# Five sums made ahead for the first feed-forward in place of eight, two of them for its first pieces, and three more for the second

## The chip, the cores and the metric

The kernel runs on one core of one Trainium2 chip. The metric is the device time of one execution in microseconds (us); lower is better. The profile's engines are TensorE (PE, its weight loads PEld), VectorE (DVE), ScalarE (ACT), GpSimd (POOL) and SyncE (SP). In this kernel SP starts the loads of weights, and POOL starts the transfers that store or fetch intermediate tensors and those that add into their target.

## The reference

One layer of a streaming encoder on 256 tokens of width 2048, all in float32. D_FF is 5632.

```python
x = x + 0.5 * swiglu(rms_norm(x), w_up1, w_down1)      # first feed-forward: FFN1
h = rms_norm(x); proj = h @ w_in                       # the middle
...                                                    # HGRN2 and RG-LRU branches, gates, out projection
x = x + cross_attention(rms_norm(x), rms_norm(mem), wq, wkv, wo)
x = x + 0.5 * swiglu(rms_norm(x), w_up2, w_down2)      # second feed-forward: FFN2
return rms_norm(x)

def swiglu(h, w_up, w_down):
    gate, up = split(h @ w_up, 2)
    return (silu(gate) * up) @ w_down
```

The keys and values of the cross attention depend on `mem` alone (256 tokens) and are computed first of all.

## The kernel before

**Split numbers.** Each float32 operand is split into a high part `h` (a copy rounded to the fast matmul type, by ScalarE, line 147) and a low part `l` (the operand minus `h`, by VectorE, line 148). A product takes three matmuls: high x high, low x high, high x low.

**Pieces.** Weights come in tiles of 128 x 2048 (1 MB), called pieces here, in one planned order: 16 pieces for the memory's values, 16 for its keys (the stage K, lines 367 and 370), FFN1, the middle, FFN2. `weights()` prepares pieces two ahead of the one in use: SP loads `raw` (three buffers, a fourth, `raw1`, in FFN1), ScalarE makes `h`, VectorE makes `l`.

**A feed-forward** has 11 groups. A group has 8 pieces of the up projection; between groups stand pieces of the down projection (two after groups 1 and 2, four after each later one). When a group ends, its sums are evicted, and its results are transposed (line 643) a few pieces later.

**Fast pieces.** Over the blocks of an up piece a Strassen-like scheme with 7 products (21 matmuls) is used in place of 8. It needs four sums of the piece's blocks, each 128 x 512: `td`, made by VectorE in lines 334, 336 and 338, then split to `th` and `tl`. A letter in the table PIECES says how a piece is prepared:

- `f`: raw is loaded, VectorE makes the sums and both low parts.
- `a`: as `f`, but the low part `l` of raw is made by ScalarE (minus raw, line 343) and by a transfer of POOL that adds the piece to it (line 344, `l<-wu`).
- `r`: the sums have been made ahead and lie in device memory. SP loads three quarters of raw (line 317) and the stored sums (line 322, `td<-t`), and VectorE makes only low parts.

The digit is the piece's number in the group. A fifth kind, "fast early", is an `f` whose sums are put into other buffers (`slot`, and raw itself), since the pool `wide` (four buffers, for `td` and `tl`) lies over the tiles of the stages before it.

**Sums made ahead.** `make_ahead` has two steps: POOL loads a piece into a buffer `prep` (line 208); some pieces later VectorE makes the sums in place (line 213, four instructions of 128 x 512) and POOL stores them (line 214). `beside(i)` runs at each prepared piece i and says when each step comes: a new load every third piece, the sums two pieces behind it. There is one `prep` buffer in the stages before FFN1, two or three in the middle, where FFN2's sums are made.

The engines' queues are in order. A scheduler fixes the order of instructions on each engine when the kernel is built, so a wait at the head of a queue holds all that stands behind it.

Of the kernel before, what the change touches and what calls it, by code (L numbers as in the profile page):

```python
# [19 lines left out]
NG = DFF // 512  # L20
# [22 lines left out]


PIECES = "f1 a3 f0 a4 f2 a5 a6 f7"
FIRST = [PIECES.replace("f2", "r2") if g in (1, 2, 4, 5, 6, 7, 8, 9) else PIECES for g in range(NG)]


def first(g):
    return [("fast", g, int(e[1])) for e in FIRST[g].split()]  # L50


def ffn_order(every=False):

    out = [("mixed" if p > 5 else "fast", 0, p) for p in range(8)] if every else first(0)  # L60
    down = [("down", 0, 1, c, 0) for c in range(4)]
    for g in range(1, NG):
        if every:
            out += [("fast", g, p) for p in (1, 3, 4, 0, 2, 5, 6, 7)]
        else:
            out += first(g)
        if g > 2 and g % 2:
            down = [("down", g - 2, 2, c, b) for c in range(4) for b in (g - 2, g - 1)]
        n = 2 if g < 3 else 4
        out, down = out + down[:n], down[n:]  # L70
    return out + [("down", NG - 2, 2, c, b) for c in range(4) for b in (NG - 2, NG - 1)]


def adds(name, e):

    return name == "ffn1" and e[0] == "fast" and f"a{e[2]}" in FIRST[e[1]]


def sums_ready(name, e):

    if name == "ffn1":
        return e[0] == "fast" and f"r{e[2]}" in FIRST[e[1]]
    made = {0: (), 1: (5, 7), 2: (3, 5, 7), 3: (3, 5, 7)}.get(e[1], (0, 3, 5, 7))
    return name == "ffn2" and e[0] == "fast" and e[2] not in made


# [1 line left out]
def block_kernel(ctx: ExitStack, tc: tile.TileContext, xT, xin, memT, vec, gfin, bgate, lruw, wu1, wd1, win, wv,  # L88
# [54 lines left out]
    done = {}  # L143
# [10 lines left out]
    plan, ahead, made_ahead, made_first = [], [], [], []  # L154
    orders = {"ffn1": ffn_order(), "ffn2": ffn_order(every=True)}

    def plan_ffn(name, wu, wd):
        for e in orders[name]:
            src = wd[e[4], e[3]] if e[0] == "down" else wu[e[1], e[2]]
            kind = "fast" if e[0] == "fast" else "plain"  # L160
            if e[0] == "down" and 0 < e[4] < NG - 1 and e[4] % 2 == 0 and e[3] % 2:
                kind = "added"
            if adds(name, e) and e not in orders[name][:2]:
                kind = "fast added"
            if kind == "fast" and (e[1] < 4 if name == "ffn2" else e in orders[name][:2]):
                kind = "fast early"
            if sums_ready(name, e):
                kind = "ready"
                t = kept.tile([P, 2048], F32, name=f"t{e[1]}_{e[2]}")
                (made_first if name == "ffn1" else made_ahead).append((src, t))  # L170
                src = src, t
            plan.append(((name,) + e, src, kind))
# [9 lines left out]
    plan_columns("k", wk, range(KT))  # L182
    first_ffn = len(plan)
    plan_ffn("ffn1", wu1, wd1)
    first_middle = len(plan)
    for hf in range(2):
# [11 lines left out]
    for g, kq in OUT_ORDER:  # L198
        plan.append((("o", g, kq), wo[g, kq], "plain"))
    first_second = len(plan)  # L200
    plan_ffn("ffn2", wu2, wd2)

    head, rest = [], {}

    def make_ahead(src, to):

        t = scoped["prep"].tile([P, 2048], F32, name="prep", tag="prep")
        nc.gpsimd.dma_start(t, src)
        yield
        b = [t[:, i * 512:(i + 1) * 512] for i in range(4)]  # L210
        with tc.issue_after(done["low"]):
            for o, x, y in ((1, 0, 1), (0, 0, 2), (2, 2, 1), (3, 3, 2)):
                dve.tensor_tensor(out=b[o], in0=b[x], in1=b[y], op=ALU.subtract)  # L213
        nc.gpsimd.dma_start(to, t)
        yield

    under_way = []

    def beside(i):

        if under_way and (i >= under_way[0][0] or "prep" not in scoped):
            next(under_way.pop(0)[1])
        if "prep" not in scoped or i < turn[0]:
            return
        if i < first_ffn:
            if made_first:
                turn[0] = i + 3 if len(made_first) > 1 else first_middle + 2
                steps = make_ahead(*made_first.pop(0))
                next(steps)
                under_way.append((i + 2, steps))  # L230
        elif made_ahead and i < first_second - 4:
            early = "scores" in scoped
            turn[0] = i + (3 if early or len(made_ahead) % 3 else 2)
            steps = make_ahead(*made_ahead.pop(0))
            next(steps)
            under_way.append((i + (2 if early or "kt" in scoped else 3), steps))

    turn = [8]
# [3 lines left out]
    def weights(*key):  # L242
        while plan and len(ahead) < 2:
            i = next(planned)
            k, src, kind = plan.pop(0)
            if i == 0:
                in_turn.enter_context(tc.manual_schedule(engines={sp.engine, act.engine, dve.engine}))
            if i == 0:
                begun.append(raw_tile())
                act.dma_start(begun[0][:, :512], in_blocks(src, 512)[:P])  # L250
            if i < len(head):
                head[i]()
            if plan and plan[0][2] == "added":
                begun.append(begin_added(plan[0][1]))
            ahead.append((k, prepare(src, kind, i if i < 4 else None)))
            if i in rest:
                rest[i]()
            beside(i)
            if i == 7:
                in_turn.close()  # L260
        k, w = ahead.pop(0)
        assert k == key, (k, key)
        return w
# [356 lines left out]
    def ffn(name, pairs, sq, then, begin=(), sums=()):  # L620
# [38 lines left out]
        for at, e in enumerate(order):  # L659
# [3 lines left out]
            if kind != "down":  # L663
# [3 lines left out]
                for i, (a, b, n) in enumerate(PRODUCTS["ready" if sums_ready(name, e) else kind]):  # L667
                    u = uses[g, n]
                    if u[0] == (p, i):
                        accs[n] = bank()  # L670
                    own, less = pairs[p]
                    products.append((accs[n], part(own, a, P) if a >= 0 else part(less, -1 - a, P), part(w[b // 4] if fast else w, b % 4, 512),
                                     u[0] == (p, i), u[-1] == (p, i)))
# [798 lines left out]
```

## Time and profile before

| | us |
|---|---|
| median of 3 runs (2517.64 to 2519.73) | 2519.39 |
| the profiled execution | 2521.97 |
| its span, from the first to the last instruction | 2520.2 |
| TensorE busy in the span | 2423.2 |
| VectorE busy in the span | 2100.6 |
| K, from its first product to FFN1's first | 99.8 to 213.1 |
| FFN1, to the last group's transposes | 213.1 to 910.7 |
| middle and FFN2 | 910.7 to 2520.2 |

A row of the profile's instructions gives the start, the duration, the engine, the line, the operation, what it writes and reads, a count, and in brackets how long the engine was idle before it and what ended that idle time. Buffer numbers are left out of names there: `td<-t` is any load of stored sums. A row of a table by stage gives for each engine its busy time and its instructions, then the clock granted to TensorE (1.00 is full), the share of time that the 16 DMA engines were busy, and their rate.

### The profile page before, as it was taken

To read this page: it belongs to the slowest core of one execution; us is meant where nothing else is said; L and a number is where in the kernel's file an instruction comes from. 1 tells how busy PE (TensorE), PEld (TensorE's weight loads), DVE (VectorE), ACT (ScalarE), POOL (GpSimd) and SP (SyncE) were. 2 spreads that over 40 slices of the span, in tenths; PEclk is the share of its full clock that TensorE was granted. 3 is DMA by queue.
4 is the path that set the end of the run, shared out by engine and by line. 5 is a ranking of instruction groups with operands and counts; after the bars stand their busy time and mean duration, and the time that the engine had idled before them with its cause. 6 is when DMAs were issued, how large, how long until landed. Compare 5 with 4: busy or idle time off the path is not lost.

```text
span 2520.2 us, 30931 instructions
## 1 busy us (share of the span) xinstructions
PE 2423.2 (96%) x12044; PEld 2004.1 (80%) x12044; DVE 2100.6 (83%) x2359; ACT 1505.3 (60%) x1549; POOL 131.7 (5%) x213
## 2 busy tenths in 40 slices
PE   9977888999999999999999999999999999999998
PEld 7866566778888788888888888888888788888887
DVE  6568788989999986777878877787799999999995
ACT  6634666767777765445456544555576666666664
POOL 0100000000000000000000000110000000000000
PEclk9988899999999999999999999999999999999999
DMA  8978677889999976877877999897787777777773
GB/s 299 340 277 281 206 228 226 266 270 283 285 283 283 272 251 261 313 273 253 322 274 286 355 351 350 320 366 289 297 299 280 276 277 274 270 274 269 279 275 150
DMA packets 109106, 711.07 MB, mean 282 GB/s; under 512 B 12128, under 2 KB 12640, under 8 KB 36256
## 3 DMA queue, kind: packets, MB, share of 16 engines
q1 hardware_dynamic: 78912, 519.56, 55.6%
q0 software_dynamic: 29904, 189.28, 24.9%
q8 instruction: 94, 1.54, 0.2%
q14 instruction: 52, 0.43, 0.0%
q10 hardware_dynamic: 144, 0.26, 0.0%
HBM read 637.62 MB, written 71.43 MB: 281 GB/s over the span
## 4 chain that ended last, share of the span: by engine, by line
PE 64%; DVE 8%; DMA 6%; issue 4%; ACT 3%; POOL 0%; ACTq 0%; DVEq 0%; POOLq 0%; SPq 0%
PE acc L603 22%; PE acc L605 11%; PE acc L367 8%; PE acc L398 6%; PE acc L392 6%; PE acc L393 6%; PE acc L370 4%; DMA raw<-wu 3%; DVE l L148 3%; DVE tl L148 2%; ACT h L147 2%; DMA l<-wu 1%; DMA td<-t 1%; PE acc L539 1%; PE acc L643 0%
## 5 line engine op out<-in xcount | busy, mean ns | idle before, releaser
L147 ACT ACTIVATE h<-raw 128x2048 fp32r<-128x2048 f32 (+3 forms) x558 | 835.3, 1522 | 616.8 <-PE acc L393 160.4
L148 DVE TENSOR_TENSOR l<-raw,h 128x2048 fp32r<-128x2048 f32 (+2 forms) x392 | 801.0, 2046 | 206.6 <-ACT h L147 205.8
L603 PE MATMUL acc<-h,xh 128*128 128x512 f32 x1230 | 486.1, 397 | 25.8 <-ACT h L147 15.2
L603 PE MATMUL acc<-h,xl 128*128 128x512 f32 x1230 | 481.4, 393 | 0.0
L603 PE MATMUL acc<-h,hidop 128*128 128x512 f32 x1408 | 356.6, 391 | 0.0
L603 PEld LDWEIGHTS acc<-h,xh 128*128 128x128 f32 x1230 | 233.2, 190 | 92.5 <-ACT h L147 41.3
L603 PEld LDWEIGHTS acc<-h,hidop 128*128 128x128 f32 x1408 | 262.4, 188 | 54.7 <-ACT h L147 1.2
L392 PE MATMUL acc<-h,ops 128*128 128x512 f32 x704 | 276.3, 392 | 0.0
L393 PE MATMUL acc<-h,ops 128*128 128x512 f32 x704 | 274.2, 389 | 0.0
L603 PEld LDWEIGHTS acc<-h,xl 128*128 128x128 f32 x1230 | 233.3, 190 | 47.0
L148 DVE TENSOR_TENSOR tl<-td,h 128x1024 fp32r<-128x1024 f32 x182 | 220.6, 1218 | 52.2 <-ACT h L147 51.7
L147 ACT ACTIVATE h<-td 128x1024 fp32r<-128x1024 f32 x182 | 190.0, 1054 | 112.5 <-PE acc L603 37.0
L367 PE MATMUL acc<-ops,h 128*128 128x512 f32 x896 | 219.1, 395 | 0.0
L605 PE MATMUL acc<-tl,xh 128*128 128x512 f32 x696 | 203.1, 395 | 1.8 <-DVE tl L148 1.8
L148 DVE TENSOR_TENSOR tl<-raw,h 128x1024 fp32r<-128x1024 f32 x166 | 196.5, 1217 | 3.1 <-ACT h L147 2.6
L213 DVE TENSOR_TENSOR prep<-prep 128x512 f32<-128x512 f32 x232 | 158.4, 687 | 48.6 <-DMA prep<-wu 45.1
L367 PEld LDWEIGHTS acc<-ops,h 128*128 128x128 f32 x896 | 165.6, 190 | 33.3
L605 PE MATMUL acc<-l,xh 128*128 128x512 f32 x534 | 158.8, 402 | 31.3 <-DMA l<-wu 24.3
L605 PE MATMUL acc<-l,hidop 128*128 128x512 f32 x704 | 188.8, 389 | 0.0
L398 PE MATMUL acc<-l,ops 128*128 128x512 f32 x704 | 174.1, 389 | 0.8 <-DVE l L148 0.8
L605 PEld LDWEIGHTS acc<-tl,xh 128*128 128x128 f32 x696 | 131.0, 190 | 32.3 <-DVE tl L148 5.6
L398 PEld LDWEIGHTS acc<-l,ops 128*128 128x128 f32 x704 | 132.1, 188 | 28.6 <-DVE l L148 1.2
(267 smaller groups left out, 2862.1 us busy)
## 6 DMA issues: line engine op xcount, KB each, us to landing
raw<-wu SPq DMA_DIRECT2D x118, 1024.0 KB, 7.0
raw<-wd SPq DMA_DIRECT2D x88, 1024.0 KB, 6.9
prep<-wu POOLq DMA_DIRECT2D x58, 1024.0 KB, 6.8
t<-prep POOLq DMA_DIRECT2D x58, 1024.0 KB, 5.4
raw<-t SPq DMA_DIRECT2D x50, 1024.0 KB, 5.5
raw<-wu SPq DMA_DIRECT2D x58, 768.0 KB, 5.9
raw<-win SPq DMA_DIRECT2D x40, 1024.0 KB, 5.1
l<-wu POOLq DMA_DIRECT2D x43, 768.0 KB, 9.7
```

Source lines behind the costliest of these rows:

```text
L147: done["high"] = act.activation(h, raw, ACT.Copy).ins
L148: done["low"] = dve.tensor_tensor(out=l, in0=raw, in1=h.bitcast(F32), op=ALU.subtract).ins
L213: dve.tensor_tensor(out=b[o], in0=b[x], in1=b[y], op=ALU.subtract)
L367: pe.matmul(acc, h[:, k * P:(k + 1) * P], xs[k], start=k == 0, stop=False)
L370: done["product"] = pe.matmul(acc[:, :T], l[:, k * P:(k + 1) * P], xs[k][:, :T], start=False, stop=k == KT - 1).ins
L392: pe.matmul(accs[t], x[:, t * P:][:, :P], h[j], start=first and j == 0, stop=False)
L393: pe.matmul(accs[t], x[:, T + t * P:][:, :P], h[j], start=False, stop=False)
L398: done["product"] = pe.matmul(accs[t], x[:, t * P:][:, :P], l[j], start=False, stop=last and j == 3).ins
L539: pe.transpose(acc[:, z * T + t * P:][:, :P], tile[:, t * 512 + (2 * y + z) * P:][:, :P], ident)
L603: pe.matmul(acc, a, b, start=start, stop=False)
L605: pe.matmul(acc, ah, bl, start=False, stop=stop)
```

## The change

FFN1 loses the stored sums of six groups (4 to 9, `r2` becomes `f2`), keeps those of groups 1 and 2, and gets them in group 3. Group 0 begins with two pieces whose sums are stored (`r1`, `r3`), in place of two "fast early" ones. So five sums are made before FFN1 where there were eight. They are started every fifth piece in place of every third, and the sums stand three pieces behind their load in place of two. FFN2 gets piece 3 of groups 5, 7 and 9 from stored sums too, three more, made in the middle, where the first of FFN2's sums follow a little closer on each other.

```diff
 PIECES = "f1 a3 f0 a4 f2 a5 a6 f7"
-FIRST = [PIECES.replace("f2", "r2") if g in (1, 2, 4, 5, 6, 7, 8, 9) else PIECES for g in range(NG)]
+FIRST = ["r1 r3 f0 a4 f2 a5 a6 f7"] + [PIECES.replace("f2", "r2") if g in (1, 2, 3) else PIECES for g in range(1, NG)]
...
-    made = {0: (), 1: (5, 7), 2: (3, 5, 7), 3: (3, 5, 7)}.get(e[1], (0, 3, 5, 7))
+    made = {0: (), 1: (5, 7), 2: (3, 5, 7), 3: (3, 5, 7)}.get(e[1], (0, 5, 7) if e[1] % 2 else (0, 3, 5, 7))
...
-            if adds(name, e) and e not in orders[name][:2]:
+            if adds(name, e):
                 kind = "fast added"
-            if kind == "fast" and (e[1] < 4 if name == "ffn2" else e in orders[name][:2]):
+            if kind == "fast" and (e[1] < 4 if name == "ffn2" else False):
                 kind = "fast early"
...
-                turn[0] = i + 3 if len(made_first) > 1 else first_middle + 2
+                turn[0] = i + 5 if len(made_first) > 1 else first_middle + 2
                 steps = make_ahead(*made_first.pop(0))
-                next(steps)
-                under_way.append((i + 2, steps))
+                with tc.issue_after(done["low"]):
+                    next(steps)
+                under_way.append((i + 3, steps))
...
-            turn[0] = i + (3 if early or len(made_ahead) % 3 else 2)
+            turn[0] = i + (2 + len(made_ahead) % 2 if early else 3 if len(made_ahead) % 3 else 2)
```

The instructions' order shows it at three places. In the rows below buffer numbers are kept; the changed kernel's lines stand one further down (L208 stays, L866 becomes L867). First POOL in K, before the change. `prep` rows are loads of pieces, `t` rows stores of sums (t6_2 is group 6, piece 2), `k` rows stores of the keys made in K, two of K's products to a store:

```order
L881 DMA k0_156<-ops_1005 128x1024
L214 DMA t5_2_98<-prep_966 128x2048
L881 DMA k1_157<-ops_1123 128x1024
L208 DMA prep_1132<-wu1 128x2048
L214 DMA t6_2_99<-prep_1132 128x2048
L881 DMA k2_158<-ops_1230 128x1024
L208 DMA prep_1310<-wu1 128x2048
L881 DMA k3_159<-ops_1349 128x1024
L214 DMA t7_2_100<-prep_1310 128x2048
```

POOL in K, after the change:

```order
L208 DMA prep_1024<-wu1 128x2048
L867 DMA v6_170<-vs_1000 128x1024
L867 DMA v7_171<-vs_1006 128x1024
L882 DMA k0_156<-ops_996 128x1024
L882 DMA k1_157<-ops_1111 128x1024
L214 DMA t1_2_97<-prep_1024 128x2048
L208 DMA prep_1296<-wu1 128x2048
L882 DMA k2_158<-ops_1221 128x1024
L882 DMA k3_159<-ops_1335 128x1024
L882 DMA k4_160<-ops_1429 128x1024
L214 DMA t2_2_98<-prep_1296 128x2048
```

Between a load and the store of its sums there stand now two or three stores of keys, where there were none or one.

Second VectorE in K, before the change, round the sum with the buffer prep_1132. `l` rows are K pieces' low parts, `sum` and `ops` rows finish K's products, `xl` and `xs` rows prepare FFN1's operand:

```order
L148 TENSOR_TENSOR l_1354<-raw_1352,h_1353 128x2048
L148 TENSOR_TENSOR xl_1184<-xs_1239,xh_1183 128x512
L213 TENSOR_TENSOR prep_1132<-prep_1132 128x512
L409 TENSOR_TENSOR sum_1292<-acc_1257,lo_1290 128x256
L213 TENSOR_TENSOR prep_1132<-prep_1132 128x512
L148 TENSOR_TENSOR xl_1190<-xs_1303,xh_1189 128x512
L213 TENSOR_TENSOR prep_1132<-prep_1132 128x512
L148 TENSOR_TENSOR l_1402<-raw_1400,h_1401 128x2048
L213 TENSOR_TENSOR prep_1132<-prep_1132 128x512
```

VectorE in K, after the change, round the fourth sum:

```order
L148 TENSOR_TENSOR l_1498<-raw_1496,h_1497 128x2048
L410 TENSOR_TENSOR sum_1427<-acc_1392,lo_1425 128x256
L434 TENSOR_TENSOR ops_1429<-sum_1427,ops_1429 128x256
L148 TENSOR_TENSOR xl_1442<-xg_1438,xh_1441 128x512
L148 TENSOR_TENSOR l_1557<-raw_1555,h_1556 128x2048
L148 TENSOR_TENSOR xl_1448<-xg_1438,xh_1447 128x512
L213 TENSOR_TENSOR prep_1296<-prep_1296 128x512
L410 TENSOR_TENSOR sum_1491<-acc_1456,lo_1489 128x256
```

The sums stand between the same kinds of rows as before, and further behind their own load: the load of prep_1296 goes out before POOL's store k2, the sums come after the product of m 8 (sum_1427, kept in ops_1429).

Third SP where FFN1's first pieces are loaded, before the change (raw_1774 is f1, raw_1844 a3, raw_1888 f0, raw1_1963 f2, raw_1925 a4):

```order
L302 DMA raw_1723<-wk 128x2048
L324 DMA raw_1774<-wu1 128x2048
L324 DMA raw_1844<-wu1 128x2048
L324 DMA raw_1888<-wu1 128x2048
L324 DMA raw1_1963<-wu1 128x2048
L324 DMA raw_1925<-wu1 128x2048
L324 DMA raw_2000<-wu1 128x2048
```

And after it (raw_1753 and raw_1755 are r1, raw_1821 and td_1823 are r3, raw_1863 is f0, raw1_1938 f2, raw_1900 a4, raw_1975 a5):

```order
L303 DMA raw_1702<-wk 128x2048
L318 DMA raw_1753<-wu1 128x1536
L323 DMA raw_1755<-t0_1_95 128x2048
L318 DMA raw_1821<-wu1 128x1536
L325 DMA raw_1863<-wu1 128x2048
L325 DMA raw1_1938<-wu1 128x2048
L325 DMA raw_1900<-wu1 128x2048
L325 DMA raw_1975<-wu1 128x2048
L323 DMA td_1823<-t0_3_96 128x2048
```

The stored sums of r3, the second piece in use, are loaded behind the raw tiles of four later pieces.

## The prediction

> **What bounds the kernel now.** First the page, for the engine that sets the end and where it rests:
>
> ```profile
> span 2520.2 us, 30931 instructions
> PE 2423.2 (96%) x12044; PEld 2004.1 (80%) x12044; DVE 2100.6 (83%) x2359; ACT 1505.3 (60%) x1549; POOL 131.7 (5%) x213
> PE   9977888999999999999999999999999999999998
> PEclk9988899999999999999999999999999999999999
> ```
>
> TensorE works 96% of the span, so a change that leaves the matmul count alone can only win its 97 us of rest and the slow clock after it. Both lie in slices 2 to 6 (63 us each). Second, the busy time by stage. I cut where K's first product starts (99.8), where the first feed-forward (FFN1) starts (213.1), and then at the transposes of line 643, which stand at the same place of each group:
>
> ```profile
> core 0: us, PE busy (x) PEld busy (x) DVE busy (x) ACT busy (x) POOL busy (x), PEclk, DMA share, GB/s
> 11.00:99.80 88.80, 88.79 (x385) 73.36 (x385) 68.22 (x89) 65.98 (x104) 4.29 (x8) 0.98 0.87 320
> 99.80:213.10 113.30, 94.86 (x513) 82.16 (x512) 68.75 (x100) 46.02 (x66) 11.72 (x22) 0.92 0.81 299
> 213.10:286.70 73.60, 55.31 (x206) 41.16 (x205) 60.32 (x69) 43.31 (x41) 4.56 (x6) 0.86 0.73 223
> 286.70:349.30 62.60, 52.08 (x214) 40.26 (x214) 54.39 (x58) 37.66 (x33) 3.45 (x4) 0.95 0.74 223
> 473.00:535.60 62.60, 60.76 (x268) 49.18 (x267) 58.15 (x60) 45.06 (x38) 4.36 (x5) 1.00 0.92 289
> 535.60:849.40 313.80, 307.74 (x1361) 251.21 (x1360) 288.87 (x295) 225.63 (x191) 21.69 (x25) 0.99 0.91 281
> 849.40:910.70 61.30, 61.30 (x274) 50.04 (x273) 58.72 (x61) 45.82 (x39) 4.36 (x5) 1.00 0.90 268
> 910.70:1852.00 941.30, 935.72 (x5457) 792.13 (x5456) 725.41 (x932) 489.69 (x586) 62.47 (x117) 1.00 0.82 304
> ```
>
> K (second row) and group 0 (third) rest 18 us each, at clocks of 0.92 and 0.86. Groups 4 to 9 (rows five and six) nearly keep up; group 10 (row seven) doesn't rest at all. Third, TensorE's instructions in time, for the waits in K and group 0, with one undisturbed pair of K's products and the stall that group 1 repeats:
>
> ```profile
> 115.20 2.18 PE L370 MATMUL acc<-ms,l 128*128 128x256 f32 x16 [0.48 <-DVE l L148]
> 148.40 3.82 PE L367 MATMUL acc<-ms,h 128*128 128x512 f32 x16
> 153.97 3.82 PE L367 MATMUL acc<-ms,h 128*128 128x512 f32 x16
> 162.95 3.78 PE L370 MATMUL acc<-ms,l 128*128 128x256 f32 x16 [5.16 <-DVE l L148]
> 188.94 5.74 PE L367 MATMUL acc<-ms,h 128*128 128x512 f32 x16 [9.97 <-ACT h L147]
> 223.68 0.79 PE L603 MATMUL acc<-h,xh 128*128 128x512 f32 x1 [9.01 <-DVE td L334]
> 247.96 1.65 PE L605 MATMUL acc<-l,xh 128*128 128x512 f32 x3 [5.04 <-DMA l<-wu]
> 306.79 1.65 PE L605 MATMUL acc<-l,xh 128*128 128x512 f32 x3 [5.84 <-DMA l<-wu]
> ```
>
> Fourth, why VectorE is late there, in its own instructions and the waits:
>
> ```profile
> 110.00 0.69 DVE L213 TENSOR_TENSOR prep<-prep 128x512 f32<-128x512 f32 x1 [9.12 <-DMA prep<-wu]
> 157.87 0.69 DVE L213 TENSOR_TENSOR prep<-prep 128x512 f32<-128x512 f32 x1 [7.34 <-DMA prep<-wu]
> 182.71 0.69 DVE L213 TENSOR_TENSOR prep<-prep 128x512 f32<-128x512 f32 x1 [11.10 <-DMA prep<-wu]
> 218.12 1.42 DVE L213 TENSOR_TENSOR prep<-prep 128x512 f32<-128x512 f32 x2 [7.85 <-DMA prep<-wu]
> DVE prep L213 <- DMA prep<-wu: 43.4, 6, 11.1
> 80.44 0.53 POOL L208 DMA_DIRECT2D prep<-wu  x1 [12.39 <-DMA t<-prep]
> 174.78 0.53 POOL L208 DMA_DIRECT2D prep<-wu  x1 [9.82 <-DMA t<-prep]
> 163.91 0.53 POOL L214 DMA_DIRECT2D t<-prep  x1 [13.62 <-DVE ops L433]
> DMA to landing us min/median/max: 4.1/8.0/12.6
> ```
>
> VectorE's queue stood 43.4 us, six times, before a sum made ahead whose load had not landed; the splits queued behind it are what TensorE waits for at 163, 189 and 224. The load is late because the one prep buffer must first be stored: load 8, sums about 3, store 8 (the last row's median for both), plus the wait of the store behind other POOL work (13.62), make 20 us and more, while a sum comes every third piece, 3 x 5.57 = 16.7 us (153.97 - 148.40 is one K piece).
>
> **The change, part by part.**
>
> *K.* 16 pieces x 5.57 = 89.1 of the window's 113.3: lost 24.2. Five sums come 5 pieces apart (27.9 us), and a sum stands 3 pieces behind its load: 16.7 us for a landing of 8, at most 12.6. By the order of the changed kernel I place them: the first sum moves back by a piece, and with it the second load from 80.44 to about 86, landed by 94 to 98, where VectorE arrives near 91; that wait of 3 to 7 us falls where 9.12 cost TensorE only 0.48 (rows at 110.00 and 115.20); the third after m 3 (99.8 + 4 x 5.57 = 122), load landed by 118; the fourth after m 8 (150), landed by 142; the fifth after m 12 (172), landed near 173. I keep 2 us of loss: -22. From below -24, from above -9 (the stall that ends at 163 and the 9.97 stay, 15). POOL carries two loads and two stores fewer between k's stores, so nothing queues there longer. The DMA engines have room: 113.3 us x 299 GB/s = 33.9 MB, less two loads and two stores (4.2 MB), plus r1's stored sums, are about 30.5 MB in 91 us, 335 GB/s, and before K they moved 320 GB/s with TensorE at 88.79 of 88.80.
>
> *Group 0.* 9 pieces of 21 matmuls lie in its window, at 61.30 / 274 = 0.224 us 42.3; lost 31.3: 18.3 of rest, 1 in transposes, the remainder slow clock. r1's parts are ready before K ends, so the 9.01 goes. What is late next is r3: its stored sums go into a wide buffer over the memory operands, free only at K's end, and SP issues them behind four loads of raw, the last of which waits for r3's own low split at K's end + 1.5. With the landing of such a load,
>
> ```profile
> raw<-wu SPq DMA_DIRECT2D x118, 1024.0 KB, 7.0
> SPq L324 <- DMA prep<-wu: 12.9, 1, 12.9
> SPq L324 <- DMA t<-prep: 7.8, 1, 7.8
> ```
>
> they land at + 8.5 and are split at + 9.5; TensorE wants them at 4.8 (one piece) + 1.4 (six matmuls) = + 6.2: 3 us of new wait, with ACT's and VectorE's work for f0 and a4 behind it. The two SP rows are a cost that goes: raw1's load stood 20.7 us behind the last sum's load and store, and a4's raw behind it, hence the 5.04. VectorE loses the whole of f1 and the sums of a3. Kept: 3 (r3), 3 (a4), 5 small waits and 5 slow clock = 16: -15. Bounds: -25 (nothing but r3 and transposes) and 0 (r3 late by as much as the 9.01).
>
> The clock here: 16 matmuls after the 9.97 took 5.74 instead of 3.82, so 1.9 lost; in the window 55.31 busy against 42.3 + 1 is 12 lost. The Trainium skill, TensorE: Matmul & The Clock Gate, Part 1: The HAM clock gate, says that the clock halves after an idle window of about 3.4 us and returns after as long a busy one; an estimate by it is 1.7 per long stall, 3.4 for group 0's two. The first row agrees, the window doesn't. By the rule no wait of 3 us would slow the clock and the sum would be 5 us better.
>
> *Groups 1 to 3.* The order is the same but for r2 in group 3; VectorE enters earlier by group 0's share, yet each such group gives it 54.39 us of work for 62.60. -2, between -6 and 0: the 5.84 is of their own making, a late copy by accumulation.
>
> *Groups 4 to 9 get f2 for r2.* Each adds a sum on VectorE and spares 0.75 MB of loading and a wait on stored sums (rows: the sums in the stretch 213 to 473, then the waits from 473 to 849.4):
>
> ```profile
> L334 DVE TENSOR_TENSOR td<-raw 128x1024 f32<-128x1024 f32 x31 | 37.6, 1215 | 0.0
> L336 DVE TENSOR_TENSOR td<-raw,td 128x512 f32<-128x512 f32 x28 | 19.1, 683 | 0.1
> L338 DVE TENSOR_TENSOR td<-raw,td 128x512 f32<-128x512 f32 x28 | 19.1, 682 | 0.1
> ACT h L147 <- DMA td<-t: 13.5, 5, 5.3
> 634.16 0.50 PE L603 MATMUL acc<-h,xh 128*128 128x512 f32 x1 [0.83 <-ACT h L147]
> ```
>
> 1.2 + 0.7 + 0.7 = 2.6 us each, 15.5 in all, on a VectorE busy 58.15 of 62.60. But group 10 already has f2: 58.72 busy, 61.30 long, no rest. The six windows take 62.60 + 313.80 = 376.4, at group 10's length 367.8: up to -8.6, since the waits on stored sums go. Above: +14, if VectorE sets the pace. Nearest is group 10; I take half, -4.
>
> *Sums for the second feed-forward.* Three more, in pairs of loads and stores (2 MB each) and 4 x 0.69 us of VectorE, in the middle: PE 935.72 of 941.30, VectorE 725, DMA at 0.82 cover them: 0 (bounds -1, +4). That cover gone, they would cost their 8 us of VectorE. What r3 gives groups 5, 7 and 9 there is 2.6 us of VectorE against 0.75 MB: 0, between -3 and +5 (a stored-sum wait of 5.3 once).
>
> Sum: -22 - 15 - 2 - 4 = -43, from the profiled execution's own 2521.97 (span 2520.2 and 1.8 around it): 2479. The median of the runs shown, 2519.39, lies 2.6 under that execution: **2476.5**, rounded 2477.
>
> **Rivals.**
> 1. r3 is late by the whole 9: group 0 gains nothing. For it: four loads ahead, and ACT and VectorE hold it ahead of f0 in order. Against: those loads are mostly in flight before. 2519.4 - 28 = 2491. Chance 0.14.
> 2. The change doesn't do what it says: loads still come late, since POOL puts them behind k's stores, and K keeps 15. Against: 27.9 us of room for a ring of some 20. 2519.4 - 43 + 13 = 2489. Chance 0.10.
> 3. Slower: VectorE passes its limit in groups 4 to 9, and they fall into the state of group 1, where a4's copy comes late each time (62.60 for 8 pieces and two down steps, 12 lost). 6 x 12 = 72 against 39: 2552. It decides from 6.5 us per group on. For it: six such groups in a row at 58.15 + 2.6 = 60.8 of 61.3. Against: group 10, and the later part of group 3, have f2 and no rest. Chance 0.05.
>
> **How the numbers follow.** My forecast has 0.69; rival 1 0.14, rival 2 0.10, rival 3 0.05, a net of nothing 0.02. Its own span, by the bounds of K and groups 0 and 4 to 9 taken together loosely, is 2460 to 2495. The range 2458 to 2502 takes in rivals 1 and 2 with some slack and leaves out rival 3. A measurement tells about 0.2%, 5 us, from no change: faster 0.93, same 0.02, slower 0.05.
>
> **What the profile after would show.** K's 16 products in about 91 us and no wait on prep of over 3 us on VectorE after 110; FFN1 starting near 191; a wait at r3 of about 3 us, by ACT h from td; transposes of group 0 near 249; groups 4 to 9 between 61.3 and 62.6 with no td<-t wait, VectorE near 60 in each; the middle unchanged at 941. I am wrong if VectorE still stands before prep, if r3's wait is over 8, or if a4's copy is waited for in groups 4 to 9.

## The result and the profile after

| | before | after |
|---|---|---|
| median of 4 runs each, us | 2518.51 (2517.59 to 2519.73) | 2475.63 (2472.92 to 2477.15) |
| span of the profiled execution, us | 2520.2 | 2473.0 |

The changed kernel takes 0.9828 of the time (95% interval 0.9811 to 0.9845), 43 us less. Forecast were 2477 us, between 2458 and 2502. The total came out; of its terms K was right, group 0 gained 8 us less than forecast and groups 4 to 9 gained 4 us more, so that their errors offset each other in part.

First the head of the page of the changed kernel, for TensorE and VectorE:

```profile
span 2473.0 us, 30918 instructions
PE 2408.2 (97%) x12044; PEld 1997.1 (81%) x12044; DVE 2100.1 (85%) x2359; ACT 1510.1 (61%) x1551; POOL 131.7 (5%) x213
PEclk9998999999999999999999999999999999999999
```

VectorE does the same work, 2100 us; TensorE is 15 us less busy for the same 12044 matmuls, because fewer ran at a slow clock. The table by stage, cut at the same events as before (K, group 0, groups 1 to 3 one by one, group 4, groups 5 to 9 together, group 10, then the middle and FFN2; the last cut is the first product of FFN2):

```profile
core 0: us, PE busy (x) PEld busy (x) DVE busy (x) ACT busy (x) POOL busy (x), PEclk, DMA share, GB/s
96.10:185.20 89.10, 89.10 (x514) 78.77 (x513) 70.46 (x100) 51.17 (x70) 9.60 (x18) 1.00 0.95 353
185.20:252.00 66.80, 51.84 (x205) 40.60 (x205) 51.91 (x57) 39.77 (x37) 4.04 (x5) 0.90 0.75 226
252.00:312.50 60.50, 50.68 (x213) 39.65 (x212) 52.86 (x56) 37.44 (x33) 3.45 (x4) 0.94 0.76 231
312.50:376.20 63.70, 54.25 (x226) 42.71 (x225) 55.38 (x59) 39.88 (x35) 3.47 (x4) 0.95 0.73 226
376.20:436.80 60.60, 52.70 (x225) 42.13 (x224) 53.18 (x55) 40.80 (x35) 3.48 (x4) 0.94 0.82 262
436.80:499.10 62.30, 61.49 (x274) 49.93 (x273) 60.39 (x63) 46.14 (x39) 4.36 (x5) 1.00 0.90 271
499.10:805.80 306.70, 306.12 (x1361) 250.13 (x1360) 299.83 (x310) 226.72 (x191) 21.74 (x25) 1.00 0.91 274
805.80:867.10 61.30, 61.30 (x274) 50.03 (x273) 58.79 (x60) 45.83 (x39) 4.35 (x5) 1.00 0.92 275
867.10:1782.90 915.80, 912.30 (x5355) 773.25 (x5354) 710.77 (x914) 474.08 (x562) 65.60 (x123) 1.00 0.83 312
1782.90:2473.00 690.10, 676.64 (x3007) 553.97 (x3005) 620.73 (x601) 440.28 (x405) 6.95 (x8) 1.00 0.75 270
```

The same two last stages of the kernel before:

```profile
910.70:1829.90 919.20, 913.62 (x5355) 773.87 (x5354) 703.73 (x902) 470.84 (x560) 62.47 (x117) 1.00 0.82 304
1829.90:2520.20 690.30, 675.98 (x3007) 554.09 (x3005) 627.19 (x610) 440.46 (x405) 6.94 (x8) 1.00 0.75 266
```

The account from these rows and those of the prediction (the start is K's first product, at 99.8 and 96.1). One cut of the prediction is put right here: before the change the transposes of group 3 begin at 472.26, and the prediction cut at 473.0, which gave groups 1 to 3 0.7 us too much and groups 4 to 9 as much too little:

| stage | before | after | difference | forecast |
|---|---|---|---|---|
| start | 99.8 | 96.1 | -3.7 | 0 |
| K | 113.3 | 89.1 | -24.2 | -22 |
| group 0 | 73.6 | 66.8 | -6.8 | -15 |
| groups 1 to 3 | 185.6 | 184.8 | -0.8 | -2 |
| groups 4 to 9 | 377.1 | 369.0 | -8.1 | -4 |
| group 10 | 61.3 | 61.3 | 0 | 0 |
| middle and FFN2 | 1609.5 | 1605.9 | -3.6 | 0 |
| sum (span) | 2520.2 | 2473.0 | -47.2 | -43 |

K now has no rest at all: busy 89.10 of 89.10 at a full clock. The instructions that answer to the stalls shown of before are these, on VectorE, SP, ScalarE, VectorE again, and TensorE:

```profile
92.43 1.42 DVE L213 TENSOR_TENSOR prep<-prep 128x512 f32<-128x512 f32 x2 [2.31 <-DMA prep<-wu]
185.48 2.05 SPq L325 DMA_DIRECT2D raw<-wu  x3
187.58 0.44 SPq L323 DMA_DIRECT2D td<-t  x1
199.76 2.00 ACT L147 ACTIVATE h<-td 128x1024 fp32r<-128x1024 f32 x2 [11.80 <-DMA td<-t]
200.85 2.36 DVE L148 TENSOR_TENSOR tl<-td,h 128x1024 fp32r<-128x1024 f32 x2 [12.43 <-ACT h L147]
200.87 0.80 PE L604 MATMUL acc<-h,xh 128*128 128x512 f32 x1 [8.72 <-ACT h L147]
223.67 1.65 PE L606 MATMUL acc<-l,xh 128*128 128x512 f32 x3 [3.02 <-DMA l<-wu]
```

The first row is the only wait of VectorE on `prep` that is left: 2.31 us, where the prediction showed 43.4 in six (45.1 in seven from 60 to 225 us). The other rows are group 0's: r3's stored sums are issued at 187.58, after three loads of raw, and are there at 199.76, 14.6 us after FFN1's start; ScalarE, VectorE and TensorE wait for them one behind the other. The last row is the wait for a4's copy, as the transfer `l<-wu` that completes a4's low part is called below.

### The profile page after: what moved, and what is told of

It reads as the page before. It is cut to its first block, busy times and chain, and to the rows that moved or that the text cites. A ratio compares the mean times of both kernels' runs of the same rounds, so it can differ in the third digit from the quotient of the medians.

```text
span 2473.0 us, 30918 instructions
## 1 busy us (share of the span) xinstructions
PE 2408.2 (97%) x12044; PEld 1997.1 (81%) x12044; DVE 2100.1 (85%) x2359; ACT 1510.1 (61%) x1551; POOL 131.7 (5%) x213
## 4 chain that ended last, share of the span: by engine, by line
PE 74%; DVE 4%; issue 3%; DMA 3%; ACT 2%; POOL 0%; ACTq 0%; POOLq 0%; DVEq 0%
PE acc L604 26%; PE acc L606 13%; PE acc L368 8%; PE acc L393 7%; PE acc L394 6%; PE acc L399 6%; PE acc L371 4%; DMA raw<-wu 2%; ACT h L147 1%; DVE l L148 1%; DMA l<-wu 1%; DVE tl L148 1%; PE acc L644 1%; PE acc L540 1%; PE acc L994 0%
## 5 line engine op out<-in xcount | busy, mean ns | idle before, releaser
L604 PEld LDWEIGHTS acc<-h,xl 128*128 128x128 f32 x1230 | 232.8, 189 | 47.2
L606 PEld LDWEIGHTS acc<-l,hidop 128*128 128x128 f32 x704 | 132.1, 188 | 27.7
```

The costliest lines, as they stand in the source:

```text
L604: pe.matmul(acc, a, b, start=start, stop=False)
L606: pe.matmul(acc, ah, bl, start=False, stop=stop)
```

## The experiments

All ratios are to the kernel before, on the same chip. Unless it says otherwise, a kernel is the changed one with the edit shown. Kernels 1 to 4 ran together, 5 to 8, and 9 to 12. The stages are from one profiled execution of each.

| kernel | median, us | ratio (95% interval) | K | group 0 | groups 1 to 3 | groups 4 to 9 | middle and FFN2 |
|---|---|---|---|---|---|---|---|
| before | 2518.51 | | 113.3 | 73.6 | 185.6 | 377.1 | 1609.5 |
| changed | 2475.63 | 0.9828 (0.9811 to 0.9845) | 89.1 | 66.8 | 184.8 | 369.0 | 1605.9 |
| 1 five_close | 2492.14 | 0.9884 (0.9869 to 0.9899) | 101.0 | 66.3 | 185.5 | 368.4 | 1609.4 |
| 2 five_lag2 | 2474.78 | 0.9814 (0.9800 to 0.9829) | 89.0 | 62.3 | 185.5 | 368.3 | 1608.0 |
| 3 eight_lag3 | 2515.31 | 0.9975 (0.9964 to 0.9985) | 109.6 | 72.9 | 185.1 | 376.2 | 1614.7 |
| 4 r3_ahead | 2469.46 | 0.9792 (0.9776 to 0.9809) | 89.0 | 54.5 | 186.9 | 368.5 | 1609.5 |
| 5 r2_in_456 | 2489.82 | 0.9873 (0.9849 to 0.9897) | 89.0 | 66.4 | 186.1 | 376.1 | 1611.3 |
| 6 ffn2_as_before | 2484.98 | 0.9854 (0.9838 to 0.9871) | 89.0 | 71.0 | 185.9 | 369.8 | 1610.7 |
| 7 early_first_pieces | 2477.11 | 0.9824 (0.9810 to 0.9839) | 89.0 | 62.2 | 185.0 | 368.3 | 1609.2 |
| 8 r1_in_123 | 2469.53 | 0.9799 (0.9784 to 0.9813) | 89.0 | 56.5 | 187.5 | 369.7 | 1608.3 |
| 9 f4_in_123 | 2463.23 | 0.9774 (0.9756 to 0.9793) | 89.0 | 54.6 | 183.8 | 369.2 | 1608.3 |
| 10 two_sums | 2466.74 | 0.9789 (0.9770 to 0.9808) | 89.0 | 54.0 | 187.2 | 369.0 | 1607.9 |
| 11 r3_ahead_ffn2_as_before | 2469.13 | 0.9796 (0.9776 to 0.9816) | 89.0 | 56.1 | 184.6 | 368.5 | 1608.2 |
| 12 r3_ahead_again | 2466.97 | 0.9791 (0.9773 to 0.9810) | 89.0 | 54.8 | 186.9 | 368.5 | 1607.6 |

**K: the number of sums, their distance, or their lag.** Three kernels. The first keeps the changed kernel's five sums at the old distance and lag:

```diff
-                turn[0] = i + 5 if len(made_first) > 1 else first_middle + 2
+                turn[0] = i + 3 if len(made_first) > 1 else first_middle + 2
-                under_way.append((i + 3, steps))
+                under_way.append((i + 2, steps))
```

> The changed kernel with its five sums started every third piece and made two pieces behind their load, as before the change; all else changed. If the room between the sums is what K gained (one prep buffer, a ring of some 20 us), the sums that now fall to the start of K wait for their loads again: VectorE stands 7 to 9 us before each of them, TensorE loses about 0.5 + 2.8 + 5.2 us of the stalls that stood there, the 9.97 late in K is gone because no sum is left there, and K takes about 97 us, the whole about 2484. If the number of sums is what counts (three loads and stores fewer for the DMA engines and POOL), K takes 89 to 91 us and the whole stays at 2476.

K took 101.0, 4 us more than expected, and the whole 2492, 8 us more. VectorE's waits on `prep` (total, times, longest, from 60 to 225 us), two sums with their waits, and the stalls of TensorE that follow:

```profile
DVE prep L213 <- DMA prep<-wu: 25.6, 4, 9.3
125.08 0.69 DVE L213 TENSOR_TENSOR prep<-prep 128x512 f32<-128x512 f32 x1 [6.77 <-DMA prep<-wu]
156.96 0.69 DVE L213 TENSOR_TENSOR prep<-prep 128x512 f32<-128x512 f32 x1 [7.71 <-DMA prep<-wu]
128.03 2.18 PE L371 MATMUL acc<-ms,l 128*128 128x256 f32 x16 [2.32 <-DVE l L148]
162.04 3.79 PE L371 MATMUL acc<-ms,l 128*128 128x256 f32 x16 [5.51 <-DVE l L148]
```

The waits on `prep` are back, and the splits behind them are late by what TensorE loses. The second kernel has the new distance with the old lag:

```diff
-                under_way.append((i + 3, steps))
+                under_way.append((i + 2, steps))
```

> The changed kernel with the sums two pieces behind their load in place of three; every fifth piece as changed. If the room of the ring decides (27.9 us between sums), VectorE waits a few us before some sums, TensorE's lead of two pieces covers it, K takes 89 to 91 us, the whole 2476. If the distance between a load and its sums decides, 2 x 5.57 = 11.1 us against landings of 5 to 12 us behind a store, VectorE's waits of 7 us and more come back, K takes 95 to 105, the whole 2482 to 2492.

K took 89.0, and VectorE didn't wait on `prep` once. Group 0 took 62.3 in place of 66.8; the last section says what differs there. The third is the kernel before, eight sums and the old distance, with the new lag:

```diff
-                under_way.append((i + 2, steps))
+                under_way.append((i + 3, steps))
```

> The kernel before with the sums three pieces behind their load in place of two, eight sums every third piece. With the ring of about 20 us against 16.7 us the loads stay late whatever the lag: VectorE still stands 30 us or more before prep in K, K takes 105 to 113 us, the whole 2508 to 2519. If the lag alone was at fault, K takes about 91 us and the whole 2495.

```profile
DVE prep L213 <- DMA prep<-wu: 30.2, 7, 9.5
```

Of the 45.1 us of waits from 60 to 225 us 30.2 stay, and K keeps 20 of its 24 us. So the lag of three pieces is neither needed nor enough. At the old distance five sums lose 12 us and eight lose 24; at five pieces apart five lose nothing. Eight at five pieces apart don't fit into the stages before FFN1 and were not tried, so as far as these runs show, the fewer sums cure K by way of the room they leave. A second `prep` buffer was not tried either.

**Group 0: r3's load.** The stored sums of r3 go into two tiles of the pool `slot`, which are free earlier than `wide`, and are issued before the loads of raw that stood ahead of them:

```diff
+            if r3:
+                third = [slot(name="td") for _ in range(2)]
+                for n, v in enumerate(third):
+                    done["sums"] = sp.dma_start(v, t[:, n * 1024:(n + 1) * 1024]).ins
...
-            sp.dma_start(raw, src)
+            with (tc.issue_after(done["sums"]) if "wide" in scoped and "raw2" not in scoped else ExitStack()):
+                sp.dma_start(raw, src)
...
-        halves = [td[:, a:a + 1024] for a in ((0,) if kind == "fast early" else (0, 1024))]
+        halves = third if r3 else [td[:, a:a + 1024] for a in ((0,) if kind == "fast early" else (0, 1024))]
```

> The changed kernel with r3's stored sums in two other buffers that are free during K (slot tiles in place of the wide tile over the memory operands), and SP's later loads of raw in FFN1 kept behind them. If r3's late sums cost what its wait shows, the 8.72 us wait goes, ScalarE and VectorE start f0 and a4 some 10 us earlier, group 0 takes about 57 to 60 us in place of 66.8, the whole 2467 to 2470. If VectorE's work or a4's copy sets group 0 anyway, the wait reappears behind it and the whole is 2474 to 2476.

Group 0 took 54.5. Its row by stage, its longest wait, and ScalarE's splits of the two halves of r3's sums:

```profile
187.52:242.00 54.48, 51.20 (x206) 39.31 (x205) 50.33 (x55) 40.12 (x37) 4.04 (x5) 0.94 0.86 272
206.78 0.96 PE L615 MATMUL acc<-l,xh 128*128 128x512 f32 x3 [0.89 <-DMA l<-wu]
189.15 1.06 ACT L147 ACTIVATE h<-td 128x1024 fp32r<-128x1024 f32 x1 [0.99 <-PE acc L613]
190.43 1.05 ACT L147 ACTIVATE h<-td 128x1024 fp32r<-128x1024 f32 x1
```

The splits wait for no load, the 8.72 is gone, and a4's copy is waited for 0.89 in place of 3.02 (the row at 206.78). Taking the wait away brought 12.3 us of group 0 in the profile, more than expected, but the span became only 4.9 us shorter: the start is 2.4 us longer there, groups 1 to 3 are 2.1 (and again in r3_ahead_again), and the stretch after FFN1 3.6. The median, 2469.46, is lower than the changed kernel's; the two ran on different occasions, and the intervals of their ratios meet (to 0.9809, from 0.9811), but against five_lag2, which ran with it, the runs don't overlap (2468.65 to 2470.47, 2473.72 to 2476.31).

Then the other half of the change for group 0, undone: its first pieces are `f1 a3` with early sums again, so that only three sums are made before FFN1:

```diff
-FIRST = ["r1 r3 f0 a4 f2 a5 a6 f7"] + [PIECES.replace("f2", "r2") if g in (1, 2, 3) else PIECES for g in range(1, NG)]
+FIRST = [PIECES] + [PIECES.replace("f2", "r2") if g in (1, 2, 3) else PIECES for g in range(1, NG)]
...
-            if adds(name, e):
+            if adds(name, e) and e not in orders[name][:2]:
-            if kind == "fast" and (e[1] < 4 if name == "ffn2" else False):
+            if kind == "fast" and (e[1] < 4 if name == "ffn2" else e in orders[name][:2]):
```

> The changed kernel with group 0's first two pieces as before (f1 and a3 of the early kind, their sums made by VectorE into slot tiles), so with three sums before FFN1 in place of five. If r1 and r3 are what made group 0 shorter (66.8 from 73.6, though r3 waits 8.7 us), group 0 takes about 69 to 74 us and the whole 2478 to 2483. If r3's late sums cost as much as the two pieces save, and the 9 us wait of before came only from the eighth sum that held VectorE, group 0 takes 58 to 63 us with early pieces and the whole is 2468 to 2473.

```profile
185.90:248.10 62.20, 51.47 (x206) 39.13 (x205) 54.12 (x61) 40.75 (x38) 4.04 (x5) 0.95 0.71 207
208.66 0.79 PE L606 MATMUL acc<-l,xh 128*128 128x512 f32 x1 [5.87 <-DMA l<-wu]
```

Group 0 took 62.2, no more than in any kernel with r1 and r3 as the change places them (62.3 to 71.0), and the ratio is the changed kernel's. So r1 and r3 as placed brought nothing. The 9.01 of the kernel before is gone here too, though f1 and a3 are made as before. Two things differ from before at that place: no sum made ahead is left there, where the last one's wait of 7.85 at 218 stood in VectorE's queue and its load and store held raw1's load back, and K ends without stalls. The runs don't tell the two apart. That the 9.01 goes isn't enough: in eight_lag3, with all eight sums, no wait at that place is over 1.5 us, but a copy comes 7.77 late and group 0 takes 72.9. With r3 on time r1 and r3 do bring something: 54.5.

**Groups 4 to 9: what stored sums cost there.** The three stored sums go to groups 4 to 6, and groups 1 to 3 make theirs:

```diff
-... PIECES.replace("f2", "r2") if g in (1, 2, 3) else PIECES ...
+... PIECES.replace("f2", "r2") if g in (4, 5, 6) else PIECES ...
```

> The changed kernel with the three stored sums of piece 2 given to groups 4, 5 and 6 in place of 1, 2 and 3; the sums before FFN1 are made at the same times. If the stored sums cost groups with four down steps a wait for their load, groups 4 to 6 take about 1 to 3 us more each again (62.5 to 65) and show td<-t waits on ScalarE; groups 1 to 3 get 2.6 us more of VectorE's work each and, since VectorE is what makes them late, take 2 to 2.6 us more each. Together 2485 to 2490. If the gain of groups 4 to 9 came from something else (an earlier or less loaded start, the clock), groups 4 to 6 stay at 61.2 to 62 and the whole is 2476 to 2484.

Groups 4 to 6 took 192.0 in place of 185.3 (62.3 + 61.8 + 61.2). ScalarE's waits on stored sums there, of which the changed kernel has none in these groups, then the row by stage, and TensorE's longest wait:

```profile
ACT h L147 <- DMA td<-t: 8.9, 3, 5.5
440.90:632.90 192.00, 186.67 (x817) 152.36 (x816) 174.36 (x179) 136.22 (x115) 13.06 (x15) 0.98 0.90 279
530.49 0.80 PE L606 MATMUL acc<-l,xh 128*128 128x512 f32 x1 [2.88 <-DMA l<-wu]
```

Groups 1 to 3 took 186.1 in place of 184.8, though VectorE makes three sums more there. So in groups 4 to 6 a stored sum costs on average 2.2 us more than making the sum. The cost is uneven: the groups took 63.2, 66.8 and 62.0, and in the middle one a copy came 2.88 late, with slow matmuls behind it. In the kernel before, with stored sums in all six, group 5 is the longest too (65.2, a copy 2.67 late). Why a stored sum costs here and, by two_sums below, nothing in groups 1 to 3 is open: here four down pieces stand behind each group and the DMA engines are at 0.90, there two behind groups 1 and 2 and the DMA engines at 0.73 to 0.82, and no run separates the two. The median rose by more than these 8 us; the profile has the rest in the start (99.3) and after FFN1 (1611.3), which the edit doesn't touch.

**Groups 1 to 3.** Three kernels, each on top of r3_ahead. One stores piece 1 in place of piece 2:

```diff
-... PIECES.replace("f2", "r2") if g in (1, 2, 3) else PIECES ...
+... PIECES.replace("f1", "r1") if g in (1, 2, 3) else PIECES ...
```

> The kernel with r3's sums loaded early (r3_ahead, 2469) and, in groups 1 to 3, piece 1 from stored sums in place of piece 2. If VectorE's work at the start of these groups (evictions, then the sums of f1) is what makes a4's copy late there by 5.7 us, taking 2.6 us of sums out ahead of it shortens each group by 2.5 to 5 us: 2456 to 2462. If the copy's own chain (ScalarE's low part behind another piece's high part, then a transfer of some 9 us) sets it, the stall stays and the whole is 2467 to 2472.

```profile
308.00 1.65 PE L615 MATMUL acc<-l,xh 128*128 128x512 f32 x3 [4.92 <-DMA l<-wu]
325.35 0.96 PE L615 MATMUL acc<-l,xh 128*128 128x512 f32 x3 [3.25 <-DMA l<-wu]
```

a4's late copy shrank from 5.7 to between 4.3 and 5.0, and a second copy was late by 3.3 and 3.4 behind it in two of the groups: no gain. The next stores nothing for groups 1 to 3, so that two sums are made in all:

```diff
-... PIECES.replace("f2", "r2") if g in (1, 2, 3) else PIECES ...
+... PIECES ...
```

> r3_ahead with only r1 and r3 made ahead for FFN1, piece 2 of groups 1 to 3 as f2. The prediction gave stored sums in groups 1 to 3 little; groups 1 to 3 took 186.1 us with f2 and 184.8 with r2 in two profiles. If r2 is worth nothing there, 2468 to 2472. If VectorE's 2.6 us per group count in full, 2475 to 2479.

It is as fast as a second run of r3_ahead beside it, the control (2466.74 against 2466.97), and groups 1 to 3 are as long (187.2 against 186.9). The three stored r2 are worth nothing that can be measured. The third takes a4's copy out: piece 4 becomes `f4`, VectorE making its whole low part:

```diff
-... PIECES.replace("f2", "r2") if g in (1, 2, 3) else PIECES ...
+... PIECES.replace("f2", "r2").replace("a4", "f4") if g in (1, 2, 3) else PIECES ...
```

> r3_ahead with a4 made as f4 in groups 1 to 3: its low part by VectorE (1.7 us) and no copy by accumulation. If a4's copy, 5.7 us late in each of these groups, is a cost of its own, the three waits for l<-wu go, each group becomes 2 to 5 us shorter, 2456 to 2464. If VectorE sets these groups, busy 53 to 55 of 62.5 us with its gap only during a4's wait, the wait moves to a split of VectorE and the whole is 2467 to 2475.

TensorE's longest wait in group 1, in the changed kernel and then in this one:

```profile
271.02 1.65 PE L606 MATMUL acc<-l,xh 128*128 128x512 f32 x3 [5.77 <-DMA l<-wu]
```

```profile
266.71 0.81 PE L615 MATMUL acc<-l,xh 128*128 128x512 f32 x2 [3.14 <-DMA l<-wu]
```

The 5.77 is gone, and the copy of a later `a` piece is waited for 3.14 (3.17 and 3.52 in the next groups). It is the fastest of the kernels: three of its four runs (2461.55 to 2465.80) lie under every run of the control (2465.24 to 2469.39), but the intervals of the ratios overlap, and kernels with the same groups 1 to 3 spread from 184.6 to 186.9 there, against 183.8 here. A gain of 3.7 us is likely, not settled.

**FFN2's three more sums.** The changed kernel without them, the middle's distances as before:

```diff
-... (0, 5, 7) if e[1] % 2 else (0, 3, 5, 7))
+... (0, 3, 5, 7))
...
-            turn[0] = i + (2 + len(made_ahead) % 2 if early else 3 if len(made_ahead) % 3 else 2)
+            turn[0] = i + (3 if early or len(made_ahead) % 3 else 2)
```

> The changed kernel without the three added sums for the second feed-forward, and with the old spacing of the sums in the middle. If the middle covers them and piece 3 gains nothing in groups 5, 7 and 9, the stages from the last transposes of FFN1 to the end take 1606 to 1610 us as in all kernels so far, the whole 2474 to 2478. If the 3.6 us that this stretch became shorter came from them, it is 1609 to 1610 and the whole 2478 to 2480; a kernel of the first batch with the new sums that took 1609 speaks against it.

Its interval overlaps the changed kernel's, but its median is 9 us higher, above both expectations, and not where the edit is: of the 12.4 us by which its span is longer, group 0 has 4.2 (71.0, with r3's wait at 10.35 and a4's at 5.22), and after FFN1 it takes 1610.7, within the 1605.9 to 1611.3 of the kernels that have the three sums. The same edit was therefore made on r3_ahead, where that wait doesn't exist, beside a second run of r3_ahead itself:

> r3_ahead without the three added sums of the second feed-forward and with the old spacing in the middle, beside r3_ahead on the same chip. If they cost and bring nothing, the same as r3_ahead within 2 us. If they bring what the first attempt (2485 against 2476) and the shorter end stretch of the changed kernel hint at, 3 to 8 us slower than r3_ahead.

> r3_ahead unchanged, as the control of these three: 2467 to 2472, group 0 near 54.5 us, no wait for r3's sums.

0.9796 (0.9776 to 0.9816) and 0.9791 (0.9773 to 0.9810), with 1608.2 and 1607.6 after FFN1: the three sums bring or cost nothing that can be measured. What made r3's wait longer in ffn2_as_before stands in the last section.

## Why the prediction was right, and where it was not

That the total came within 2 us of the forecast is partly luck. The stages for which something was forecast gave 39.9 us in place of 43, with 8 us too little in group 0 and 1 in groups 1 to 3, and 4 too much in groups 4 to 9 and 2 in K; 7.3 us came at the start and after FFN1, where nothing was forecast; and the two profiled executions lie 4.4 us further apart than the medians.

*K* (forecast -22, measured -24.2). The mechanism stands: the ring of one buffer needs more than the 16.7 us between sums, and VectorE's queue holds the splits behind a load that is late. The first three experiments show that the distance does it, not the lag. One wait of 2.31 was left where 3 to 7 were placed, and it cost TensorE nothing. The rate forecast for the DMA engines, 335 GB/s, was 353, at a share of 0.95.

*Group 0* (forecast -15, measured -6.8). Here the step failed that put r3's stored sums at 8.5 us after K's end: SP issued them 2.4 after it in place of 1.5, behind three loads of raw that went out in the 2.05 us before, and they needed 12.1 us to land where I took the median of a load, 7.0:

```profile
raw<-wu SPq DMA_DIRECT2D x5, 1024.0 KB, 7.4
td<-t SPq DMA_DIRECT2D x1, 1024.0 KB, 12.1
```

These are the issues from 165 to 210 us, with their time from issue to landing. The median is one over loads that TensorE's pace spaces out; this one stood fourth in a burst of 1 MB loads. That the burst makes it slow is my reading: r3_ahead changed its place in the queue and its buffer at once, and shows only that the two together take the wait away.

What bunched the loads is in the trace, and it is a second step that failed: the prediction took SP's wait of raw1's load for the last sum as a cost that goes. It shrank from 20.7 us, but SP still stood 7.4 us before the first of the three loads, until the last sum's store had landed, 9.3 us after its issue at 176.21 and so 0.3 us after K's end:

```profile
SPq L325 <- DMA t<-prep: 7.4, 1, 7.4
176.21 0.53 POOL L214 DMA_DIRECT2D t<-prep  x1 [4.78 <-DVE prep L213]
t<-prep POOLq DMA_DIRECT2D x1, 1024.0 KB, 9.3
```

So the wait was 8.7, not 3, over the 8 that I had named as proving me wrong, and rival 1's mechanism came true. Its price was wrong all the same. Against before, the long wait shrank by 0.3 only, but a4's by 2.0, the small ones by 1.0 and TensorE's busy time by 3.5, which makes the 6.8; the rival had left all of these as they were.

The sum's base was wrong too. The window doesn't hold nine pieces of 21 matmuls but 204 matmuls of FFN1, nearly ten pieces, before and after (its rows count 206 and 205 instructions); at 0.224 they take 45.7 us and not 42.3. Above these 45.7, 21.1 us were kept and not 16: the two waits 8.7 + 3.0 in place of 3 + 3, small waits 3.2 in place of 5, and 6.1 of busy time (51.84 less 45.7), slow clock for the most part, in place of 5. What I gave VectorE for f1 and a3 that it needn't make was worth nothing (early_first_pieces).

On the clock: the matmuls after the 8.72 and the 3.02 ran at about half speed until these two rows, 12 matmuls from 200.87 on and 7 from 223.67 on:

```profile
206.15 0.40 PE L604 MATMUL acc<-h,xh 128*128 128x512 f32 x1
226.73 0.39 PE L604 MATMUL acc<-h,xh 128*128 128x512 f32 x1
```

At 0.224 each the 12 and the 7 would take 2.7 and 1.6 us; they took 5.28 and 3.06. So the two waits cost 2.6 and 1.5 us of slow clock. A shorter wait was followed by it as well: here are the three low-part matmuls of a piece without a wait in the changed kernel, and behind a wait of 2.35 in five_lag2:

```profile
188.36 0.84 PE L606 MATMUL acc<-l,xh 128*128 128x512 f32 x3
```

```profile
222.31 1.65 PE L606 MATMUL acc<-l,xh 128*128 128x512 f32 x3 [2.35 <-DMA l<-wu]
```

The Trainium skill, TensorE: Matmul & The Clock Gate, Part 1: The HAM clock gate, puts the slow clock behind an idle window of about 3.4 us; the same section says that the window runs free, and waits of 3.02 and 2.35 were followed by slow matmuls here. By the estimate of 1.7 for each long wait, the two would have cost 3.4; the rows show 4.1. The prediction's 12 us of slow clock in the window before came from the nine pieces; with 45.7 it is 9.6.

*Groups 1 to 3* (-2, -0.8): as argued; a4's late copy stayed (5.77, 5.85, 5.75).

*Groups 4 to 9* (-4, -8.1). At group 10's length they would have given -8.6 by the prediction's cut, -9.3 by the right one; taking half of that was the error. VectorE is at 60.0 a group there (299.83 over five groups), not held by it, and no load of stored sums is waited for. r2_in_456 shows the price of putting them back. Rival 3 did not come: with VectorE at 60.4 of 62.3 in group 4 a copy is waited for 0.81, in group 5 one for 0.57, and none in the others. By the letter this is a sign that I had named as proving me wrong; by its size, 1.4 us in all against 12 a group, it is not what the rival priced.

*FFN2's sums* (0): right, by kernels 11 and 12.

The -3.7 at the start and -3.6 after FFN1 have no step in the prediction, and I count them as spread between executions, which the runs make likely and don't prove: over the experiments the start lies between 95.3 and 99.3, and at 98.5 and 95.3 for r3_ahead and r3_ahead_again, one kernel run twice; the stretch after FFN1 lies between 1607.6 and 1611.3 but for eight_lag3 (1614.7), so that the changed kernel's 1605.9 is the lowest of all, and the three sums in it make no difference. With them the account is 47, where the medians differ by 43: the execution profiled before lies 3.5 above its median, the one after 0.9 below.

Rival 2, loads still late behind k's stores, is excluded by the 2.31.

## What to carry to other kernels

An operation prepared ahead on an in-order engine is only free if its input has landed when its turn comes; check the period of the whole ring (load, compute, store, and queueing before each) against the distance at which it is started, since everything queued behind it pays. Price a load by the burst in which it is issued, not by the median over the kernel: the first load that a new stage needs should be issued before the bulk ones, and into a buffer that is free before the stage begins; and look for what releases the bulk loads, here a store that was to land first, since what is held together goes out together. Work precomputed to spare an engine pays only where that engine ends the wait: three of the five sums here could go without loss.

## What the runs showed that I had not expected

The same load of r3's sums, behind the same loads in SP's queue, took 8.7 us to land in five_lag2, 12.1 in the changed kernel and 13.2 in ffn2_as_before, and TensorE's wait was 5.34, 8.72 and 10.35; group 0 went from 62.3 over 66.8 to 71.0. The last two kernels differ only in the middle and FFN2, and still group 0 differs by more than most of the terms that were forecast. With the load moved ahead, group 0 stayed between 54.0 and 56.5 in six kernels:

```profile
td<-t SPq DMA_DIRECT2D x1, 1024.0 KB, 8.7
```

```profile
td<-t SPq DMA_DIRECT2D x1, 1024.0 KB, 13.2
```

The first of these is the issue in five_lag2, the second in ffn2_as_before. The traces show where the three part: SP holds raw1's load, and all loads behind it, until the last sum's store has landed. With the lag of two that store landed 5.8 us before K's end, and the three loads of raw ahead of r3's sums were spread over 8.2 us; in the changed kernel it landed 0.3 us after K's end and in ffn2_as_before 1.4 after, and the same loads went out within 2.1 and 1.5 us. In r2_in_456 the store landed 0.9 before K's end, and r3's sums took 12.8 to land. So the lag of three, which K didn't need, is likely to have put that store in the way of group 0; these are single profiles, and the medians of five_lag2 and the changed kernel don't differ (2474.78 and 2475.63). Nor is it the whole: in five_close, where all stores are done long before, r3's sums took 11.5 to land and the wait was 8.46. Why the store itself landed later in ffn2_as_before is open.

The DMA engines ran K at 0.95 and 353 GB/s, and r3_ahead's at 0.97 and 356, with TensorE at rest for nothing: a high load on them alone didn't make K's pieces late.
